# Moving the low weight parts and the rotation of a two-block transformer kernel to VectorE, and pairing the first two outputs of each residual projection

## The chip, the cores and the metric

The kernel runs on one core of a Trainium2 chip. The metric is the device time of one execution in microseconds (us): the median of three runs is 2573.86 us (2573.84 to 2576.16). A change of less than 0.2%, about 5 us, can hardly be told from none.

## The reference

Two blocks work on one sequence of 512 tokens with 1024 channels, all in float32. The first block mixes three branches (gated linear attention "GLA" with 4 heads, a short convolution, sliding-window attention), gates and merges them, and runs a feed-forward network. The second block has two layers, each with sparse attention (an indexer picks the top keys), a gated recurrence ("HGRN") with 4 heads, a merge of both, and a feed-forward network. Cut to what matters here:

```python
def first_block(x, ...):
    u = rmsnorm(h, g_mix); z = u @ w_in
    o = gla_chunked(q, k, v, log_a)          # q*exp(b-b_ref), k*exp(b_ref-b), chunks of 64
    merged = gate0 * (o @ w_gla_o) + gate1 * (conv @ w_conv_o) + gate2 * (swa @ w_swa_o)
    h = h + merged @ w_o
    h = h + (silu(hid[..., :D_FF]) * hid[..., D_FF:]) @ w_down
def second_block(x, ...):
    for l in range(2):
        proj = rmsnorm_2(x, norm_mix[l]) @ w_in[l]
        aq = apply_rope(rmsnorm_2(aq, q_norm), cos, sin)     # the same for ak; iq and ik without norm
        y_attn = dsa_attention(aq, ak, av, iq, ik, iw)       # top 128 keys of each query by an index score
        y_hgrn = hgrn2_chunked(q_h, k_in, v_h, log_f)
        x = x + (sig(ga) * (y_attn @ w_proj_attn) + sig(gb) * (y_hgrn @ w_proj_hgrn)) @ w_out
        x = x + (silu(g) * u) @ w_ffn_out

def apply_rope(x, cos, sin):
    x1, x2 = x[..., :half], x[..., half:]
    return concatenate([x1 * cos - x2 * sin, x2 * cos + x1 * sin])
```

## The kernel before

**Matmuls.** The kernel keeps float32 accuracy by splitting both operands in a high part (rounded to the fp32r type) and a low part (the rest). A product is then three matmuls: weight low by input high, weight high by input low, high by high. `project` does this for one output tile of 128 channels by 512 tokens, over 8 slices ("K tiles") of 128 input channels (22 for the down projections): 24 matmuls into one PSUM tile `mm`, of which there are four. `project_tokens` has the tokens on the partitions: it fills all four `mm` tiles at once, with 12 matmuls for each K tile.

**Weights.** `weights` loads a float32 tile `wraw` by a DMA on SyncE's queue, ScalarE copies it to fp32r (`whi`, line 149), and an engine subtracts that from the raw weights (`wlo`, line 152). Of each of the three tiles there are three buffers of 512 columns (`wraw`: 1024). One `whi`/`wlo` pair holds four K tiles of `project`, or one K tile of `project_tokens`. The engine for `wlo` comes from the list `self.lows`, in turn: `mixing()` sets GpSimd, GpSimd, VectorE; `feeding()` sets VectorE alone; while the index and `hv` projections are written, GpSimd and VectorE take turns; from the last gates of each final merge until the next `feeding()` GpSimd alone has it. In the profile GpSimd is POOL, VectorE DVE, ScalarE ACT, TensorE PE.

**Order.** Every engine executes its instructions in order. The order is made when the program is built: a scheduler walks through the instructions as written, with a priority, and places each where its model of the engines says that it can go; weight preparation and the reading of PSUM (`evict`) are written at high priority. The stages of the second block are written one after the other (`ORDER`: index and `hv` projections, index rotation, keys, key rotation, queries, values, query rotation, then selections and attention blocks, and HGRN behind them), but selection, attention and HGRN are interleaved on the engines.

**Rotation.** `rope` multiplies by a cosine table (GpSimd, line 799), takes two half-width products with a sine table (VectorE, lines 800 and 801) and adds (GpSimd, line 802). `rotate` does so for the four token tiles of keys (`akx`) or queries (`aqx`), while `rsqrt` (lines 229 to 233, ten small dependent operations on 128x32) makes the norm on VectorE, which then multiplies (line 825). The index rotation (line 802 into `idxr`, then the copy in line 858 on VectorE) has 320 columns in each token tile.

**GLA heads.** `gla_head` has three operations on GpSimd: lines 444, 447 (halves of `lvx`) and 454 (`rE`).

**HGRN heads.** `hgrn_head` goes back and forth between VectorE (lines 493, 497, 511) and GpSimd (lines 486, 494, 495) over seven levels.

**Residual.** `merge` makes eight tiles of merged channels and splits each in `mgh` (ScalarE, line 211) and `mgl` (VectorE, line 212). `residual` then calls `project` for each of eight output tiles; the K tiles of one output are these eight merged tiles, in order. Three residual projections have 8 K tiles (`w_o` and `w_out` in two layers), three have 22.

## Time and profile before

| | us |
|---|---|
| median of 3 runs | 2573.86 |
| the profiled execution, own time | 2573.17 |
| its span, first to last instruction | 2571.4 |
| PE busy | 2496.6 (97%) |
| DVE busy | 1366.3 (53%) |
| ACT busy | 1008.3 (39%) |
| POOL busy | 772.2 (30%) |

The profile shows one execution. "Busy" is the share of time in which an engine has at least one instruction under way; matmuls overlap, so a matmul's own duration (0.39 us) is longer than the distance from one to the next. The span falls into stages, of which these are spoken of below (in us from the start): GLA heads with sliding-window attention 100 to 250; the merge and the first residual projection around 450 to 500; layer 0 of the second block with the index stage near 900, the two rotations 941 to 1000, selection, attention and HGRN 1000 to 1200, and the merge after that; layer 1 with the same stages from 1740, 1784 to 1845 and 1850 to 2050. The rest is feed-forward, where PE is never idle.

### The profile page before, as it was taken

The page shows a single profiled execution, that of the slowest core. Times are in us where ns is not written, and L with a number is a line of the kernel's source. Part 1 is how long each engine was busy: PE and PEld are TensorE (multiplying, and loading weights), DVE is VectorE, ACT ScalarE, POOL GpSimd, SP SyncE. Part 2 cuts the span into 40 slices and gives each one's busy share as a digit, 9 for nine tenths or more (in the row PEclk, how much of TensorE's full clock was granted, in tenths as well). Part 3 has the DMA queues.
Part 4 walks back from the last instruction along what each step waited for, and adds up shares of the span by engine and source line. Part 5 has one row for each costly group of instructions (what it writes and reads, how often), then busy time and mean ns, then how long its engine had stood idle before and what let it go on. Part 6 is the DMA issues. An engine that isn't in the chain of part 4 may idle for free.

```text
span 2571.4 us, 31562 instructions
## 1 busy us (share of the span) xinstructions
PE 2496.6 (97%) x11742; PEld 2038.5 (79%) x11742; DVE 1366.3 (53%) x2572; ACT 1008.3 (39%) x1830; POOL 772.2 (30%) x672
## 2 busy tenths in 40 slices
PE   9999999999999998999999999999899999999999
PEld 7877888888888876777888888887677788888887
DVE  4675222477774547996244444333799724444432
ACT  5633333444443334443343333334454333433321
POOL 4234334511101254443351111015544435211100
PEclk9999999999999999999999999999999999999999
DMA  4112232322223222111222222322111032222232
GB/s 137 58 53 81 94 99 93 107 91 98 93 94 97 91 77 71 50 37 44 99 95 98 98 93 95 99 89 90 66 50 45 26 99 97 95 99 98 92 107 88
DMA packets 67434, 217.66 MB, mean 85 GB/s; under 512 B 7744, under 2 KB 8640, under 8 KB 67280
## 3 DMA queue, kind: packets, MB, share of 16 engines
q1 hardware_dynamic: 67280, 215.65, 25.3%
q8 instruction: 92, 1.51, 0.2%
q14 instruction: 62, 0.51, 0.1%
HBM read 213.52 MB, written 2.10 MB: 84 GB/s over the span
## 4 chain that ended last, share of the span: by engine, by line
PE 80%; DVE 12%; issue 3%; ACT 2%; POOL 2%; DMA 0%; SPq 0%; DVEq 0%; ACTq 0%; POOLq 0%
PE mm L194 23%; PE mm L195 23%; PE mm L193 23%; PE mm L168 2%; PE mm L169 2%; PE mm L170 2%; DVE wlo L152 1%; DVE score L885 1%; PE at L935 1%; PE at L923 1%; DVE m L884 1%; DVE rsq_w L232 1%; POOL hG L495 1%; PE at L239 1%; DVE rsq_w L231 1%
## 5 line engine op out<-in xcount | busy, mean ns | idle before, releaser
L149 ACT CAST whi<-wraw 128x512 fp32r<-128x512 f32 (+3 forms) x824 | 502.3, 610 | 1177.8 <-PE mm L195 949.9
L194 PE MATMUL mm<-xl,whi 128*128 128x512 f32 x1920 | 758.0, 395 | 0.0
L193 PE MATMUL mm<-xh,wlo 128*128 128x512 f32 x1920 | 757.3, 394 | 0.0
L195 PE MATMUL mm<-xh,whi 128*128 128x512 f32 x1920 | 755.8, 394 | 0.0
L152 DVE TENSOR_TENSOR wlo<-wraw,whi 128x512 fp32r<-128x512 f32 (+2 forms) x533 | 390.2, 732 | 508.3 <-ACT whi L149 505.6
L152 POOL TENSOR_TENSOR wlo<-wraw,whi 128x512 fp32r<-128x512 f32 (+2 forms) x291 | 377.4, 1297 | 747.7 <-ACT whi L149 705.6
L195 PEld LDWEIGHTS mm<-xh,whi 128*128 128x128 f32 x1920 | 361.2, 188 | 73.6 <-issue 1.7
L194 PEld LDWEIGHTS mm<-xl,whi 128*128 128x128 f32 x1920 | 361.1, 188 | 73.4 <-issue 1.7
L193 PEld LDWEIGHTS mm<-xh,wlo 128*128 128x128 f32 x1920 | 361.1, 188 | 72.3 <-issue 0.7
L193 PE MATMUL mm<-acth,wlo 128*128 128x512 f32 x528 | 205.4, 389 | 0.0
L194 PE MATMUL mm<-actl,whi 128*128 128x512 f32 x528 | 205.4, 389 | 0.0
L195 PE MATMUL mm<-acth,whi 128*128 128x512 f32 x528 | 205.4, 389 | 0.0
L733 POOL TENSOR_TENSOR fg<-fg,rstd 128x512 f32<-128x512 f32 x44 | 56.6, 1287 | 425.9 <-ACT fg L732 425.9
L168 PE MATMUL mm<-wlo,xh 128*128 128x512 f32 (+2 forms) x384 | 147.0, 383 | 34.6 <-DVE wlo L152 23.1
L170 PE MATMUL mm<-whi,xh 128*128 128x512 f32 (+2 forms) x384 | 144.8, 378 | 0.0
L169 PE MATMUL mm<-whi,xl 128*128 128x512 f32 (+2 forms) x384 | 144.4, 376 | 0.1
L202 DVE TENSOR_TENSOR gate<-mm,rstd 128x512 f32<-128x512 f32 x56 | 38.7, 691 | 151.2 <-PE mm L195 150.4
L277 POOL TENSOR_TENSOR acc<-acc,sq 128x512 f32<-128x512 f32 x39 | 58.8, 1508 | 199.3 <-ACT sq L274 198.3
L168 PEld LDWEIGHTS mm<-wlo,xh 128*128 128x128 f32 x384 | 73.6, 192 | 54.5 <-DVE wlo L152 26.4
L193 PEld LDWEIGHTS mm<-acth,wlo 128*128 128x128 f32 x528 | 99.1, 188 | 20.6
L194 PEld LDWEIGHTS mm<-actl,whi 128*128 128x128 f32 x528 | 99.1, 188 | 20.6
L195 PEld LDWEIGHTS mm<-acth,whi 128*128 128x128 f32 x528 | 99.1, 188 | 20.6
(356 smaller groups left out, 3336.4 us busy)
## 6 DMA issues: line engine op xcount, KB each, us to landing
wraw<-in_w_ffn_in SPq DMA_DIRECT2D x88, 512.0 KB, 3.2
wraw<-in_w_gate SPq DMA_DIRECT2D x56, 512.0 KB, 3.2
wraw<-in_w_in SPq DMA_DIRECT2D x52, 512.0 KB, 3.2
wraw<-in_w_up SPq DMA_DIRECT2D x44, 512.0 KB, 3.2
wraw<-in_w_tok SPq DMA_DIRECT2D x32, 512.0 KB, 3.2
wraw<-in_w_ffn_out SPq DMA_DIRECT2D x32, 512.0 KB, 3.5
wraw<-in_w_down SPq DMA_DIRECT2D x16, 512.0 KB, 3.5
wraw<-in_w_po SPq DMA_DIRECT2D x32, 256.0 KB, 2.6
```

The lines of the kernel that those rows point to most:

```text
L149: nc.scalar.copy(wh, raw[:, k:k + m, :])
L152: eng.tensor_tensor(wl, raw[:, k:k + m, :], wh.bitcast(F32), op=OP.subtract)
L168: nc.tensor.matmul(ps[t][:, 0:w], xh, wl, start=i == 0, stop=False)
L169: nc.tensor.matmul(ps[t][:, 0:w], xl, wh, start=False, stop=False)
L170: nc.tensor.matmul(ps[t][:, 0:w], xh, wh, start=False, stop=i == KD - 1)
L193: nc.tensor.matmul(ps, wl, xh, start=i == 0, stop=False)
L194: nc.tensor.matmul(ps, wh, xl, start=False, stop=False)
L195: nc.tensor.matmul(ps, wh, xh, start=False, stop=i == n - 1)
L202: self.nc.vector.tensor_tensor(out, ps, other, op=OP.mult)
L231: nc.vector.tensor_tensor(w, v, y, op=OP.mult)
L277: (nc.vector if d % 2 and len(acc) > 1 else nc.gpsimd).tensor_tensor(a, a, sq, op=OP.add)
L733: nc.gpsimd.tensor_tensor(g, g, self.rstd, op=OP.mult)
```

## The change

The change does four things. (1) `feeding()` is called before the GLA heads, and the calls of `mixing()` and the special list for the index and `hv` projections are gone, so that from the GLA heads on all `wlo` subtractions go to VectorE, but for the ends of the three final merges and the residual projections behind them, which stay on GpSimd. Of 291 such instructions on GpSimd 73 stay there (25 of them before the GLA heads), and 218 go to VectorE. (2) Both GpSimd operations of `rope` go to VectorE: 48 instructions. (3) The three GpSimd operations of `gla_head` go to VectorE: 12 instructions. (4) `residual`, where it has 8 K tiles, makes its first two outputs together in the new `project_pair`: K tiles 0 to 3 of the first output, 0 to 3 of the second, 4 to 6 of the first, 4 to 6 of the second, then K tile 7 of both. Their weights come in four DMAs of 256 KB where two of 512 KB stood.

```diff
+    def project_pair(self, srcs, X):
+        nc = self.nc
+        n = len(X)
+        pss = [self.mm() for _ in srcs]
+        ws = [[] for _ in srcs]
+
+        def products(j, ks):
+            for i in ks:
+                (wh, wl), (xh, xl) = ws[j][i], X[i]
+                nc.tensor.matmul(pss[j], wl, xh, start=i == 0, stop=False)
+                nc.tensor.matmul(pss[j], wh, xl, start=False, stop=False)
+                nc.tensor.matmul(pss[j], wh, xh, start=False, stop=i == n - 1)
+
+        for k in range(0, n, 4):
+            for j, src in enumerate(srcs):
+                ws[j] += self.weights(src[:, k:k + 4, :], 4)
+                products(j, range(k, min(k + 4, n - 1)))
+        for j in range(len(srcs)):
+            products(j, (n - 1,))
+        return pss
...
-        nc.gpsimd.tensor_tensor(Xc[:, :, 0:64], mid, Bc[:, :, 0:64], op=OP.subtract)
+        nc.vector.tensor_tensor(Xc[:, :, 0:64], mid, Bc[:, :, 0:64], op=OP.subtract)
...
-        nc.gpsimd.tensor_tensor(Xc[:, :, 0:64], Xc[:, :, 0:64], kc[:, :, 0:64], op=OP.mult)
+        nc.vector.tensor_tensor(Xc[:, :, 0:64], Xc[:, :, 0:64], kc[:, :, 0:64], op=OP.mult)
...
-        nc.gpsimd.tensor_tensor(E, E, q, op=OP.mult)
+        nc.vector.tensor_tensor(E, E, q, op=OP.mult)
...
         ygla = []
+        self.feeding()
         for hd in range(4):
...
     def residual(self, src, X, scale=1.0):
+        got = {}
+
         def update(d):
-            ps = self.project(src[d], X)
+            if len(X) == KD and d < 2:
+                if d == 0:
+                    got.update(enumerate(self.project_pair([src[0], src[1]], X)))
+                ps = got.pop(d)
+            else:
+                ps = self.project(src[d], X)
...
-        nc.gpsimd.tensor_tensor(o, xv, b(C, 64), op=OP.mult)
+        nc.vector.tensor_tensor(o, xv, b(C, 64), op=OP.mult)
...
-        nc.gpsimd.tensor_tensor(out, o, o2, op=OP.add)
+        nc.vector.tensor_tensor(out, o, o2, op=OP.add)
...
         for c in ORDER:
-            self.mixing()
-            if c in "xh":
-                self.lows = [nc.gpsimd, nc.vector]
...
         for l in range(2):
-            self.mixing()
             M = self.second_mix(l, X)
```

The order of the instructions moves with it. On DVE at the key rotation of layer 0 (`akss` is the sum of squares, `akx` a token tile of the keys, `tabC` and `tabS` the cosine and sine tables) there stood before:

```order
L813 TENSOR_REDUCE akss<-asq 128x8 x2
L800 TENSOR_TENSOR rope_7750<-akx,tabS 128x8x32
L813 TENSOR_REDUCE akss<-asq 128x8 x2
L801 TENSOR_TENSOR rope_7750<-akx,tabS 128x8x32
L820 TENSOR_SCALAR akss<-akss 128x32
L800 TENSOR_TENSOR rope_7757<-akx,tabS 128x8x32
L152 TENSOR_TENSOR wlo<-wraw,whi 128x512
L229 TENSOR_SCALAR rsq_y<-akss 128x32
L801 TENSOR_TENSOR rope_7757<-akx,tabS 128x8x32
```

and now (the shifted line numbers 842, 828, 829, 830, 831 are 813, 799, 800, 801, 802 of before):

```order
L842 TENSOR_REDUCE akss<-asq 128x8 x2
L152 TENSOR_TENSOR wlo<-wraw,whi 128x512
L842 TENSOR_REDUCE akss<-asq 128x8 x2
L828 TENSOR_TENSOR rope_7753<-akx,tabC 128x512
L849 TENSOR_SCALAR akss<-akss 128x32
L829 TENSOR_TENSOR rope_7754<-akx,tabS 128x8x32
L152 TENSOR_TENSOR wlo<-wraw,whi 128x512
L250 TENSOR_SCALAR rsq_y<-akss 128x32
L830 TENSOR_TENSOR rope_7754<-akx,tabS 128x8x32
L252 TENSOR_TENSOR rsq_w<-akss,rsq_y 128x32
L828 TENSOR_TENSOR rope_7760<-akx,tabC 128x512
L152 TENSOR_TENSOR wlo<-wraw,whi 128x512
```

The cosine products and sums have joined DVE's row, and a `wlo` stands in every third to ninth place, eight from the first sum of squares to the end of the rotation.

On PE at the first residual projection (`mgh_3900` is the last of the eight merged tiles) the first output ended, and the second began, like this before:

```order
L193 MATMUL mm_3905<-mgh_3875,wlo_3913 128x512
L194 MATMUL mm_3905<-mgl_3876,whi_3912 128x512
L195 MATMUL mm_3905<-mgh_3875,whi_3912 128x512
L193 MATMUL mm_3905<-mgh_3900,wlo_3913 128x512
L194 MATMUL mm_3905<-mgl_3901,whi_3912 128x512
L195 MATMUL mm_3905<-mgh_3900,whi_3912 128x512
L193 MATMUL mm_3946<-mgh_3611,wlo_3950 128x512
```

and now the last tile is taken by both, one behind the other:

```order
L207 MATMUL mm_3906<-mgh_3875,wlo_3961 128x512
L208 MATMUL mm_3906<-mgl_3876,whi_3960 128x512
L209 MATMUL mm_3906<-mgh_3875,whi_3960 128x512
L207 MATMUL mm_3905<-mgh_3900,wlo_3946 128x512
L208 MATMUL mm_3905<-mgl_3901,whi_3945 128x512
L209 MATMUL mm_3905<-mgh_3900,whi_3945 128x512
L207 MATMUL mm_3906<-mgh_3900,wlo_3961 128x512
```

So 42 matmuls stand ahead of the first that reads the last merged tile, where 21 stood.

On PE at the start of layer 0's first merge (`yhh` and `yhl` are the HGRN heads' outputs, `aL`, `aPT` and `av` belong to an attention block, `rS` and `AT` to a HGRN head) the merge began behind all attention work before:

```order
L407 MATMUL at<-rS,hf 128x128
L405 MATMUL at<-hv,AT 128x128
L407 MATMUL at<-rS,hf 128x128
L193 MATMUL mm<-xh,wlo 128x512
L194 MATMUL mm<-xl,whi 128x512
L195 MATMUL mm<-xh,whi 128x512
```

and now attention and a HGRN head still run among the merge's first products (line 960 is 931 of before, 964 is 935, 426 is 405, 428 is 407):

```order
L193 MATMUL mm<-yhh,wlo 128x512
L428 MATMUL at<-rS,hf 128x128
L426 MATMUL at<-hv,AT 128x128
L960 MATMUL at<-csts,aL 128x128 x4
L428 MATMUL at<-rS,hf 128x128
L426 MATMUL at<-hv,AT 128x128
L428 MATMUL at<-rS,hf 128x128
L194 MATMUL mm<-yhl,whi 128x512
```

In both layers the end of selection, attention and HGRN (a whole HGRN head in layer 0, two in layer 1) has moved in among the products of the first merge.

## Rows read from the trace of the kernel before

**Rows 1.** The page's part 1: busy us (share of the span) xinstructions
```profile
PE 2496.6 (97%) x11742; PEld 2038.5 (79%) x11742; DVE 1366.3 (53%) x2572; ACT 1008.3 (39%) x1830; POOL 772.2 (30%) x672
```

**Rows 2.** Waits of PE, whole span: us in total, times, longest
```profile
PE mm L168 <- DVE wlo L152: 23.1, 7, 7.7
PE mm L168 <- POOL wlo L152: 7.3, 4, 2.7
PE at L464 <- POOL lvx L447: 3.5, 4, 1.1
PE at L437 <- DVE gD L434: 3.3, 3, 1.1
```

**Rows 3.** Windows: length, PE, PEld, DVE, ACT, POOL busy (instructions), PEclk, DMA, GB/s
```profile
941.00:1000.00 59.00, 46.73 (x194) 36.09 (x193) 45.00 (x59) 21.33 (x47) 37.65 (x26) 0.91 0.18 63
1000.00:1200.00 200.00, 190.69 (x1088) 148.74 (x1087) 172.05 (x437) 97.63 (x207) 87.17 (x98) 1.00 0.13 44
1200.00:1310.00 110.00, 110.00 (x488) 90.58 (x487) 35.02 (x63) 36.61 (x60) 39.51 (x31) 1.00 0.30 96
1784.00:1845.00 61.00, 47.31 (x202) 36.95 (x201) 44.92 (x59) 21.51 (x48) 38.17 (x27) 0.94 0.20 69
1850.00:2050.00 200.00, 190.31 (x1075) 147.60 (x1075) 176.86 (x454) 100.31 (x208) 89.57 (x97) 0.99 0.12 41
100.00:250.00 150.00, 140.96 (x761) 116.45 (x760) 94.73 (x225) 60.80 (x131) 52.59 (x44) 1.00 0.18 61
```

**Rows 4.** Timeline of DVE in the key rotation: start, us, engine, line, operation
```profile
958.10 1.28 DVE L231 TENSOR_TENSOR rsq_w<-akss,rsq_y 128x32 f32<-128x32 f32 x1
959.30 0.41 DVE L801 TENSOR_TENSOR rope<-akx,tabS 128x256 f32<-128x256 f32 x1
959.64 0.18 DVE L232 SCALAR_TENSOR_TENSOR rsq_w<-rsq_w,rsq_y 128x32 f32<-128x32 f32 x1
...
961.26 1.20 DVE L232 SCALAR_TENSOR_TENSOR rsq_w<-rsq_w,rsq_y 128x32 f32<-128x32 f32 x1
```

**Rows 5.** Timeline of POOL in the same microseconds
```profile
957.76 1.57 POOL L802 TENSOR_TENSOR akx<-rope,rope 128x512 f32<-128x512 f32 x1
...
961.14 1.27 POOL L152 TENSOR_TENSOR wlo<-wraw,whi 128x512 fp32r<-128x512 f32 x1
```

**Rows 6.** Timeline of PE behind the query rotation; in brackets idle time and releaser
```profile
993.49 0.79 PE L168 MATMUL mm<-wlo,xh 128*128 128x512 f32 x1 [7.69 <-DVE wlo L152]
994.09 0.63 PE L169 MATMUL mm<-whi,xl 128*128 128x512 f32 x1
...
996.64 0.41 PE L169 MATMUL mm<-whi,xl 128*128 128x512 f32 x1
```

**Rows 7.** Timeline of DVE in the index stage of layer 0
```profile
904.57 0.83 DVE L858 COPY idxr<-idxr 128x64 f32<-128x64 f32 x1 [0.75 <-POOL idxr L802]
905.32 0.68 DVE L152 TENSOR_TENSOR wlo<-wraw,whi 128x512 fp32r<-128x512 f32 x1
```

**Rows 8.** Timeline of PE behind that subtraction
```profile
906.06 0.50 PE L168 MATMUL mm<-wlo,xh 128*128 128x512 f32 x1 [2.95 <-DVE wlo L152]
```

**Rows 9.** Timeline of PE at the first residual projection's last K tile
```profile
473.52 0.50 PE L193 MATMUL mm<-mgh,wlo 128*128 128x512 f32 x1 [0.93 <-ACT mgh L211]
474.25 0.50 PE L194 MATMUL mm<-mgl,whi 128*128 128x512 f32 x1 [0.22 <-DVE mgl L212]
```

**Rows 10.** Timeline of DVE in a GLA head
```profile
154.16 1.71 DVE L434 TENSOR_TENSOR gD<-gD,gk 128x512 f32<-128x512 f32 x1
```

**Rows 11.** Line 152 from 1000 to 1200 us: count, ns min/median/max
```profile
L152 POOL TENSOR_TENSOR wlo<-wraw,whi x22: 1259/1287/1457, 1001.5 to 1187.7; 128x512 fp32r<-128x512 f32 x22
...
L152 DVE TENSOR_TENSOR wlo<-wraw,whi x10: 674/682/1221, 1007.4 to 1169.1; 128x512 fp32r<-128x512 f32 x10
```

**Rows 12.** Waits of DVE and of POOL, 1000 to 1200 us
```profile
DVE wlo L152 <- ACT whi L149: 8.1, 1, 8.1
...
POOL wlo L152 <- ACT whi L149: 81.7, 17, 13.6
```

## The prediction

> **What bounds the kernel now.** I read the page's first part first: PE is busy in 2496.6 of 2571.4 us [rows 1]. So everything that the change can win lies in the 74.8 us in which PE is idle, and in stretches in which PE runs at a lower clock; everything it can lose is new idle time of PE. The list of what PE waits for says whose fault the idle time is [rows 2]: 30.4 us are waits of the first matmul of a token projection (line 168) for low weight parts, 23.1 of them for VectorE's; 3.5 and 3.3 us are GLA heads waiting for `lvx` and `gD`. The busy times by stretch say where [rows 3]: the two rotation stretches lose 59.00 - 46.73 = 12.3 and 61.00 - 47.31 = 13.7 us; selection, attention and HGRN ("the dense stretches") lose 9.3 and 9.7 us; the GLA stretch 9.0; the first merge of layer 0 (1200 to 1310) nothing.
>
> Why VectorE is late in the rotations is seen in single instructions. The same small operation on 128x32 takes 0.18 us at one time and 1.20 us at another [rows 4], and at the slow times GpSimd has a two-input operation under way (1.57 us from 957.76, 1.27 us from 961.14 [rows 5]): VectorE's operation ends when GpSimd's does. So the ten small steps of the norm, which are alone worth some 2 us, are stretched behind one GpSimd operation after another, and the `wlo` that PE wants stands behind them in VectorE's row. PE then waits 7.69 us in one piece [rows 6]. And it pays once more: the matmuls behind that gap start 0.425 us apart (994.09 to 996.64, six steps) where a dense stretch has 110.00 us / 488 = 0.225 us [rows 3, 6]; that is the lower clock level of the two, 1.2 instead of 2.4 GHz, after idle time. The stretches' mean granted clock is 0.91 and 0.94 [rows 3].
>
> The Trainium skill has a rule for what rows 4 and 5 show ("SBUF — State Buffer", "Who interferes with whom"): a VectorE instruction with two SBUF inputs contends with a GpSimd instruction that reads SBUF, and the later one is blocked entirely, not slowed. The trace agrees: 1.20 us beside GpSimd against 0.18 us without.
>
> **The change, part by part.** Forecasts are made against the profiled execution, 2573.2 us (span 2571.4 and 1.8 around it); it lies 0.7 us under the median of the runs, which I neglect.
>
> (a) The rotations of keys and queries. GpSimd loses the cosine products, the sums and the `wlo`, so that only zero fills are left on it here. What VectorE now has in one rotation: 24 wide operations (4 sums of squares, 4 cosine products, 4 sums, 4 norm products, 8 `wlo`), 8 half-width ones and 11 small ones. A wide one takes 0.68 us [rows 11]; successive ones overlap by about 0.07 us (the half-width one of 0.41 us at 959.30 is followed at 959.64 [rows 4]), so 0.61. The sum: 24 x 0.61 + 8 x 0.34 + 11 x 0.20 = 14.6 + 2.7 + 2.2 = 19.5 us. PE has meanwhile one token projection to do: 8 K tiles of 12 matmuls, 96 x 0.225 = 21.6 us. So VectorE keeps up, by 2 us only, provided that the `wlo` come in time. The new order puts a `wlo` in every third to ninth place; the longest piece between two (two wide, two half-width and four small operations, and the `wlo` itself) is about 3.3 us, against 2.7 us in which PE uses up one K tile, and three buffers let VectorE run ahead. So I take nearly all of the 26.0 us of idle time, and the lower clock behind it: six steps x 0.2 us = 1.2 us, at three places in the trace (959, 994 and 1836 us; one stands in the rows), 3.6. Of these 29.6 us I leave 1.6 for the evacuation of the four PSUM tiles. **Gain 28 us**; bounds 14 (every second gap stays) and 29.6.
>
> (b) The index rotation and the index and `hv` weights. At 905.32 a `wlo` stands behind a copy that waited 0.75 us for GpSimd's sum [rows 7], the last of several such exchanges, and PE waits 2.95 us for it [rows 8]. On one engine the exchange is gone. Line 168's waits of 30.4 us [rows 2] are 26.0 in the rotations, so at most 4.4 us are left for these stages. **Gain 3.5 us**; bounds 0 and 4.4. The low parts of the index weights now stand among the norm's small steps at each layer's start; there they replace GpSimd operations that block VectorE, so I set nothing for them.
>
> (c) The GLA heads. `gD` takes 1.71 us [rows 10] where an undisturbed wide operation takes 0.68 [rows 11], and PE waits 3.3 us for it in three heads and 3.5 us for `lvx` from GpSimd in four [rows 2]. Now `lvx` has two more operations of 0.34 us on VectorE and `rE` one of 0.61, but the order puts `gD` ahead of `dec`, `rD` and the scan. VectorE's load there is 94.7 of 150 us [rows 3], so the moved `wlo` have room. **Gain 4 us** of the 6.8; bounds -2 (VectorE's row has a `wlo` ahead of `gD`) and 7.
>
> (d) The pair of residual outputs. PE waits 0.93 and 0.22 us for the last merged tile [rows 9]; with 21 matmuls more in between (21 x 0.225 = 4.7 us) it is there. The same gap stands at three residual projections, one in the rows: 3 x 1.15. The four `mm` tiles suffice (two are held), the DMA bytes are the same. **Gain 3 us**; bounds 0 and 3.5.
>
> (e) The dense stretches. Here the change costs. 22 `wlo` per stretch go from GpSimd to VectorE [rows 11] (I take the same number in layer 1): 22 x 0.61 = 13.4 us on top of 172.05 and 176.86 us of 200 [rows 3], so 185.5 and 190.3. PE's own busy time there is 190.7 and 190.3 us [rows 3]: VectorE becomes as long as PE. Two things relieve it: the new order pushes the last HGRN heads and attention blocks in among the first merge's products, where VectorE has 35.0 of 110 us [rows 3], and GpSimd's 22 operations of 1.29 us no longer block VectorE or stand in front of GpSimd's own HGRN steps. Bounds: a gain of half of the idle 19.0 us, 9.5; a loss of all of the moved work, 2 x 13.4 = 27 us. I take a small **loss of 4 us**, 2 per layer: the load is equal to PE's and not above it, and the row of PE is filled with merge products.
>
> (f) Merges and feed-forward. In the merge stretch PE has no idle time, VectorE 35.0 of 110 us [rows 3]; more `wlo` there cost nothing. The feed-forward already has all `wlo` on VectorE.
>
> Sum: 28 + 3.5 + 4 + 3 - 4 = 34.5; 2573.2 - 34.5 = 2538.7, say **2539 us**, 1.4% faster.
>
> **The rivals.**
>
> A. VectorE becomes the bound in the dense stretches. Priced by the upper bound of (e): 27 us lost instead of 4, 2562 us. For it: 96% of PE's time before any wait inside a row that alternates with GpSimd and PE. Against it: the spill into the merge.
>
> The Trainium skill speaks for A ("Perfetto Trace Analysis", "Optimizing Scalar/DVE Operations"): where VectorE is saturated, offloading work, even to GpSimd, may make sense, though the shared read port may take the gain away. By its first half the `wlo` of these stretches belong on GpSimd, which is rival A's time; the trace bears out the second half, in rows 4 and 5.
>
> B. Slower than before: VectorE's row is held up by the `wlo` themselves. An engine executes in order, and a `wlo` waits for ScalarE's `whi`, which waits for PE to free a buffer. On GpSimd these waits are 81.7 us in the first dense stretch, 17 of 22 instructions [rows 11, 12]; there they hurt little, on VectorE they would hold the selection and HGRN behind them. If half of 81.7 us came onto PE's path in each of two layers, 82 us would be lost: 2539 + 82 - 4 = 2617. It ends slower than before from 47% of that, 38 us for both layers together. Against it: VectorE already has 10 `wlo` in that stretch, and waited for `whi` once, 8.1 us [rows 12], at the stretch's start.
>
> C. The rotation doesn't do what it should: VectorE's row stays the wall. If a whole rotation without `wlo` (19.5 - 8 x 0.61 = 14.6 us) ran ahead of the next `wlo`, three buffers would cover 3 x 2.7 = 8.1 us, and PE would wait 6.5 us in each of four rotations: 26 us, so that (a) gives 3.6 instead of 28: 2563 us. Against it stands the order, which interleaves.
>
> **How the numbers follow.** My forecast has 0.72, A 0.13, C 0.07, B 0.05; 0.03 is for causes that I don't see. The range reaches down to 2525 (half of the dense idle time gone: 2539 - 4 - 9.5) and up to 2559 (most of A, or half of (a) with (c) and (b) near zero). A run can tell about 0.2%, 5 us, from no change: faster than 2569 holds my forecast, A and C, 0.91; the same 0.04; slower 0.05.
>
> **What would show it.** In the profile after, the PE gaps of 7.69 us and the half-clock matmuls behind the rotations are gone, the 128x32 steps all take about 0.2 us, and line 168's waits for `wlo` fall from 30 us to under 5. The gap ahead of the last merged tile is gone at all three places. POOL's busy time falls by about 218 x 1.29 + 48 rotation operations, some 340 us, with PE's unchanged within 10. VectorE is over 90% busy in the dense stretches. I am wrong if PE's idle time in the dense stretches doubles (A), if VectorE waits there for `whi` in many pieces (B), or if line 168 still waits for `wlo` behind rotation work (C).

## The result, and the profile after

The changed kernel takes 2531.8 us (median; 2530.59 to 2532.61) beside 2574.39 for the kernel before (now four runs): a ratio of 0.9834, 95% interval 0.9818 to 0.9849, so 1.7% faster. The forecast was 2539 with a range of 2525 to 2559. The profiled execution has a span of 2530.5 us, 40.9 less than the 2571.4 of the kernel before.

The page's part 1 of the kernel after answers [rows 1] (busy us, share of the span, instructions):

```profile
PE 2493.2 (99%) x11742; PEld 2041.8 (81%) x11742; DVE 1454.1 (57%) x2850; ACT 1003.2 (40%) x1826; POOL 424.3 (17%) x394
```

POOL's busy time has fallen by 347.9 us (some 340 were expected), PE's has changed by 3.4. PE's idle time has halved, from 74.8 to 37.3 us (span less busy time). What PE still waits for, in the view of its waits over the whole span (us in total, times, longest), answers [rows 2]:

```profile
PE at L530 <- DVE lvx L514: 6.6, 16, 1.2
PE at L260 <- DVE ron L436: 6.1, 4, 2.8
PE mm L193 <- DVE wlo L152: 3.4, 3, 1.5
PE mm L193 <- ACT yhh L232: 3.0, 2, 1.5
...
PE mm L168 <- DVE wlo L152: 0.9, 1, 0.9
```

The 30.4 us for which line 168 waited are 0.9, and these stand at the kernel's start, as they did before. The waits for `gD` and for GpSimd's `lvx` of the GLA heads are gone. At the top stand waits of the HGRN heads (`lvx`, the normalised output `ron`, and its high part `yhh`) and of the products around them (`wlo` at line 193).

The rotation of the keys in the timeline of DVE (start, us, engine, line, operation) answers [rows 4]. Every 128x32 step takes 0.18 us now, between wide operations of 0.68 us and a `wlo` every few places:

```profile
933.84 0.18 DVE L252 TENSOR_TENSOR rsq_w<-akss,rsq_y 128x32 f32<-128x32 f32 x1
933.94 0.69 DVE L828 TENSOR_TENSOR rope<-akx,tabC 128x512 f32<-128x512 f32 x1
934.54 0.68 DVE L152 TENSOR_TENSOR wlo<-wraw,whi 128x512 fp32r<-128x512 f32 x1
935.15 0.18 DVE L253 SCALAR_TENSOR_TENSOR rsq_w<-rsq_w,rsq_y 128x32 f32<-128x32 f32 x1
935.25 0.68 DVE L831 TENSOR_TENSOR akx<-rope,rope 128x512 f32<-128x512 f32 x1
```

Where the 40.9 us come from is read by stages. A stage runs from its first matmul to the next stage's, and its length comes from windows laid on these points. "Token" is index, `hv`, keys, queries and values with their rotations; "dense" is selection, attention, HGRN and the first merge, up to the second merge's first product on the attention's output. Here are the windows of the kernel after, token and dense stage of layer 0, then of layer 1 (length; PE, PEld, DVE, ACT and POOL busy; granted clock; the DMA columns behind it are not used):

```profile
863.20:973.80 110.60, 109.49 (x529) 91.30 (x528) 71.09 (x180) 48.45 (x100) 2.03 (x4) 1.00 0.29 94
973.80:1252.80 279.00, 266.34 (x1401) 209.51 (x1400) 214.79 (x520) 120.19 (x243) 56.52 (x71) 0.98 0.17 56
...
1696.40:1804.90 108.50, 107.81 (x519) 90.09 (x518) 62.89 (x152) 47.12 (x98) 1.05 (x2) 1.00 0.29 96
1804.90:2083.00 278.10, 266.01 (x1401) 210.54 (x1400) 214.73 (x520) 119.69 (x243) 62.10 (x76) 0.98 0.17 55
```

The same four stages of the kernel before:

```profile
874.50:1006.00 131.50, 114.45 (x529) 92.66 (x529) 74.60 (x131) 48.49 (x100) 66.94 (x58) 0.96 0.23 79
1006.00:1277.00 271.00, 261.69 (x1401) 207.05 (x1400) 196.17 (x482) 119.09 (x243) 107.42 (x114) 1.00 0.17 58
1722.00:1848.70 126.70, 111.25 (x519) 90.62 (x518) 64.05 (x103) 47.14 (x98) 65.64 (x58) 0.97 0.24 82
1848.70:2122.50 273.80, 264.11 (x1401) 208.26 (x1400) 196.73 (x482) 124.73 (x247) 113.98 (x118) 0.99 0.17 56
```

So the token stages win 20.8 and 18.2 us by the first matmuls' own times (39.0 together), and the dense stages lose 8.0 and 4.3. The first stage, up to the first residual, wins 10.0; the three residual stages 1.4, 1.3 and 1.4. Feed-forward and second merges stay within 0.1 us.

The dense stages' loss is seen at the end of the last HGRN head. The timeline of PE of the kernel after, layer 0 (idle time and releaser in brackets):

```profile
1182.85 0.40 PE L195 MATMUL mm<-yhh,whi 128*128 128x512 f32 x1
1186.07 0.66 PE L260 MATMUL at<-csts,ron 128*128 128x128 f32 x4 [2.82 <-DVE ron L436]
1188.22 1.65 PE L193 MATMUL mm<-yhh,wlo 128*128 128x512 f32 x3 [1.49 <-ACT yhh L232]
1189.66 0.63 PE L194 MATMUL mm<-yhl,whi 128*128 128x512 f32 x1
1190.09 0.63 PE L195 MATMUL mm<-yhh,whi 128*128 128x512 f32 x1
...
1193.81 0.80 PE L193 MATMUL mm<-xh,wlo 128*128 128x512 f32 x1 [1.38 <-DVE wlo L152]
```

PE has run out of other products, waits 2.82 us for `ron` and 1.49 for its high part, and the matmuls behind that start 0.43 us apart instead of 0.23: half clock. In the window from 1187 to 1199 us the granted clock (behind POOL's busy time) is 0.57:

```profile
1187.00:1199.00 12.00, 9.40 (x24) 6.97 (x25) 5.07 (x8) 2.87 (x5) 0.00 (x0) 0.57 0.18 66
```

### The profile page after: what moved, and what is told of

Same layout as the page of the kernel before. It is cut to its first block, busy times and chain, and to the rows that moved or that the text cites. A ratio compares the mean times of both kernels' runs of the same rounds, so it can differ in the third digit from the quotient of the medians.

```text
span 2530.5 us, 31512 instructions
## 1 busy us (share of the span) xinstructions
PE 2493.2 (99%) x11742; PEld 2041.8 (81%) x11742; DVE 1454.1 (57%) x2850; ACT 1003.2 (40%) x1826; POOL 424.3 (17%) x394
## 4 chain that ended last, share of the span: by engine, by line
PE 91%; DVE 4%; ACT 2%; issue 1%; POOL 1%; DMA 0%; SPq 0%; DVEq 0%; POOLq 0%; ACTq 0%
PE mm L193 25%; PE mm L194 25%; PE mm L195 25%; PE mm L168 3%; PE mm L169 3%; PE mm L170 3%; PE at L964 1%; PE at L952 1%; PE at L260 1%; PE at L960 1%; PE at L530 1%; DVE hf L518 1%; DVE wlo L152 1%; PE at L580 0%; PE at L609 0%
## 5 line engine op out<-in xcount | busy, mean ns | idle before, releaser
L152 DVE TENSOR_TENSOR wlo<-wraw,whi 128x512 fp32r<-128x512 f32 (+2 forms) x751 | 537.4, 716 | 551.0 <-ACT whi L149 547.3
L152 POOL TENSOR_TENSOR wlo<-wraw,whi 128x512 fp32r<-128x512 f32 (+1 forms) x73 | 95.8, 1315 | 91.7 <-ACT whi L149 73.8
L714 POOL TENSOR_TENSOR acc<-acc,gate 128x512 f32<-128x512 f32 x20 | 33.7, 1687 | 342.3 <-DVE gate L709 342.3
```

The costliest lines, as they stand in the source:

```text
L152: eng.tensor_tensor(wl, raw[:, k:k + m, :], wh.bitcast(F32), op=OP.subtract)
L714: eng.tensor_tensor(acc[m], acc[m], g, op=OP.add)
```

## The experiments

The theories after the result were two. First, in the token stages GpSimd's two-input operations and VectorE's shut each other out, and the low parts behind them come late; the rivals are the order and the exchange of results inside the rotation. Second, the dense stages pay for VectorE's load; the rivals are the low parts' own waits, and the last head's place. Here are the stage lengths (us) of all kernels; "first" ends at the first residual.

```
                       first  token 0  dense 0  token 1  dense 1   median
before                 467.7    131.5    271.0    126.8    273.8   2574.4
after                  457.7    110.7    279.0    108.5    278.1   2531.8
rotation alone         468.0    111.8    271.1    109.4    273.8   2536.6
low parts alone        467.3    119.2    279.1    113.2    278.7   2556.7
GLA and pair alone     464.0    133.5    270.9    127.8    274.7   2567.6
after + 8 reads        459.0    125.1    279.5    121.7    277.3   2560.9
after + fills          458.8    110.6    277.0    108.6    280.0   2533.1
after, merges swapped  458.4    110.6    277.6    108.5    279.6   2531.6
after, HGRN lows back  457.8    110.7    269.3    108.6    268.9   2513.9
  and load elsewhere   458.2    110.7    269.3    108.4    269.4   2517.4
  and load in place    458.6    110.6    277.2    108.5    274.1   2526.7
  heads 1, 2 only      458.0    110.6    271.9    108.5    272.7   2521.6
  heads 3, 4 only      458.4    110.7    269.3    108.5    270.4   2515.8
  all on GpSimd        458.8    110.7    269.0    108.5    270.1   2514.9
```

Each row is one profiled execution. Kernels whose dense stages have the same work as the kernel after (low parts alone, 8 reads, fills) lie between 277.0 and 279.5 us in layer 0 and between 277.3 and 280.0 in layer 1, so there a difference of under 3 us says little. The token stages with both parts of the change and no added reads agree within 0.2 us; those of the kernel before and of "GLA and pair alone", which have the same work, differ by 2.0 and 1.0.

**The parts alone.** The rotation's two operations on VectorE, in the kernel before:

```diff
-        nc.gpsimd.tensor_tensor(o, xv, b(C, 64), op=OP.mult)
+        nc.vector.tensor_tensor(o, xv, b(C, 64), op=OP.mult)
...
-        nc.gpsimd.tensor_tensor(out, o, o2, op=OP.add)
+        nc.vector.tensor_tensor(out, o, o2, op=OP.add)
```

> The kernel before with one part of the change alone: the rotation's cosine product and its sum (lines 799 and 802) on VectorE; the low weight parts stay where they were, two of three on GpSimd. Theory (two-input GpSimd operations block VectorE, and the exchange between the two engines inside a rotation makes the low parts late): the 39.0 us that the change takes from the two token-projection stages need both parts, since each remaining low part on GpSimd (1.29 us) still blocks VectorE; some 15 to 25 us of the 39.0 come, so 2548 to 2559 us, and PE's idle time in the two stages falls from 32.5 to 12 to 20 us. Rival (the exchange of the rotation alone is the cause): nearly all of the 39.0 comes, 2535 to 2540 us, idle under 5 us. Rival (the low parts alone are the cause): under 5 us come, 2569 us or more. In all three the GLA stage (15.4 us idle), the residuals (45.1 us each) and the dense stretches (9.3 and 9.7 us idle) stay as before.

Measured: 2536.56 us, ratio 0.9852 (0.9838 to 0.9867). The token stages win 37.1 of the 39.0 us, so the first rival was right and my sum of two halves wrong. The low parts that stay on GpSimd cost 1.9 us in both layers together. It is not that they don't collide: VectorE's 128x32 steps still take up to 1.3 us here. The timeline of POOL in this kernel shows a `wlo` that is held up for 4.53 us:

```profile
976.14 4.53 POOL L152 TENSOR_TENSOR wlo<-wraw,whi 128x512 fp32r<-128x512 f32 x1 [1.23 <-ACT whi L149]
```

The timeline of DVE in the same kernel and the same microseconds shows operation upon operation, the next one started before the last has ended, up to 979.5 us. The one behind that takes 1.67 us instead of 0.68, while GpSimd's `wlo` ends (976.14 + 4.53 = 980.67):

```profile
976.37 1.28 DVE L825 TENSOR_TENSOR aqx<-aqx,rsq_y 128x512 f32<-128x512 f32 x2
977.57 0.68 DVE L802 TENSOR_TENSOR aqx<-rope,rope 128x512 f32<-128x512 f32 x1
978.17 0.41 DVE L800 TENSOR_TENSOR rope<-aqx,tabS 128x256 f32<-128x256 f32 x1
978.51 0.68 DVE L825 TENSOR_TENSOR aqx<-aqx,rsq_y 128x512 f32<-128x512 f32 x1
979.11 0.41 DVE L801 TENSOR_TENSOR rope<-aqx,tabS 128x256 f32<-128x256 f32 x1
979.55 1.67 DVE L802 TENSOR_TENSOR aqx<-rope,rope 128x512 f32<-128x512 f32 x1
```

So here it is GpSimd that is kept out first, and PE had enough other `wlo` meanwhile: its wait at line 168 for `wlo` is 0.9 us, as in the kernel after.

The low parts alone, in the kernel before (the first line stands ahead of the GLA heads):

```diff
+        self.feeding()
...
         for c in ORDER:
-            self.mixing()
-            if c in "xh":
-                self.lows = [nc.gpsimd, nc.vector]
...
         for l in range(2):
-            self.mixing()
```

> The kernel before with the other part alone: every low weight part on VectorE wherever the change puts it there; rotation, GLA operations and residuals as before. Theory: GpSimd has only the rotation's two operations per head group left, but VectorE's low parts stand behind them in its row; in the token stages 10 to 20 of the 39.0 us come. The dense stretches lose what the change loses there, 12.2 us in the sum of both layers, since the same low parts move. The GLA stage gains some 3 of its 9.7 us. In all 2565 to 2575 us: the same as before. Rival (the low parts alone are the cause): token stages gain 30 us or more and the whole 2545 to 2552. Rival (VectorE's row is now held up by GpSimd's sums, and no GpSimd low part can be served meanwhile): token stages lose, and the whole is over 2580 us.

Measured: 2556.71 us, ratio 0.9932 (0.9917 to 0.9946), under the 2565 of the theory. The token stages win 25.9 us, more than the 10 to 20 of the theory and less than the rival's 30. With 37.1 for the rotation alone the two sum to 63 where both together give 39.0: either one takes away most of the loss. What the theory said is seen, though smaller: low parts stand behind stretched steps. PE's waits at line 168 in this kernel are 9.5 us:

```profile
PE mm L168 <- DVE wlo L152: 9.5, 7, 2.4
...
PE at L464 <- POOL lvx L447: 6.7, 3, 2.3
```

and 128x32 steps take up to 1.33 us, as GpSimd's sums run beside them. In the dense stages this kernel loses 8.1 and 4.9 us: the whole change's loss there (8.0 and 4.3) is the low parts'.

The GLA operations and the pair of outputs, in the kernel before (lines 444, 447 and 454 on VectorE, and `project_pair`):

> The kernel before with the two parts that lie in separate stages: the three operations of a GLA head on VectorE (seen in the first stage, up to the first residual), and the pair of residual outputs (seen in the three residual stages). Theory for the first stage: its 9.7 us of gain come from the waits for gD and lvx, so from these three operations; 5 to 9 us here. Rival: they come from the low parts of that stage, which stay on GpSimd here; then under 3 us. The residuals: 1.3 us each, 3.9 in all, as with the whole change. Everything else as before. In all 2561 to 2566 us by the theory, 2567 to 2571 by the rival.

Measured: 2567.64 us, ratio 0.9974 (0.9964 to 0.9983). The residual stages are 43.9 us each, as in the kernel after: the pair is worth 1.4 us a time. The first stage wins 3.7 us, between theory and rival; the low parts alone win 0.4 there, both together 10.0. Each takes away one of the two waits of [rows 2] and leaves or lengthens the other. Of the GLA operations alone the view of PE's waits shows

```profile
PE at L458 <- DVE gD L455: 3.7, 3, 1.3
```

(3.3 us before), and with the low parts alone the wait for `lvx` is 6.7 us, as shown above (3.5 before). Most of the gain comes only when both are gone. Why `gD` is late with VectorE's three operations alone was not followed further.

**The shared reads.** Useless work on the changed kernel, once in each key and query projection, on a scratch tile that has been read:

```diff
             nc.vector.reduce_sum(ss[:, t * 8:(t + 1) * 8], sq, axis=AX.X)
+            if t == NT - 1:
+                c = self.cos2[:, 0, None, :].to_broadcast([P, 8, 64])
+                nc.gpsimd.tensor_tensor(sq, sq, c, op=OP.mult)
+                for _ in range(7):
+                    nc.gpsimd.tensor_tensor(sq, sq, c, op=OP.mult)
```

> The changed kernel with useless work added: after the last sum of squares of each key and query projection, GpSimd multiplies a scratch tile by a cosine table eight times in place (two-input operations on 128x512 which read SBUF; some 1.3 to 1.7 us each, 10 to 14 us a rotation), while VectorE does the rotation. Nobody waits for the result. In the kernel before, the rotation's own eight GpSimd operations took 11 to 13 us there. Theory (GpSimd's reads of SBUF block VectorE, and this alone makes the low parts late): VectorE's 19.5 us a rotation and these 12 make 31 where PE has 21.6; the token stages, 110.7 and 108.5 us, grow by 10 to 20 us in the sum of both, and the whole is 2542 to 2552. Rival (it is the exchange inside the rotation, VectorE waiting for GpSimd's sum and GpSimd for VectorE's products, and not the port): VectorE stretches, but PE waits under 2 us, and the whole is 2531 to 2535.

In the control the last line is `nc.gpsimd.memset(sq, 0.0)`, seventeen times.

> The control for the run with eight useless GpSimd multiplications: at the same place one such multiplication and seventeen zero fills of the same tile, which write SBUF and read nothing (0.52 us each for 128x512 in the kernel before, 9 us in all), useless as well. Theory (what blocks VectorE is a GpSimd operation that reads two inputs): no loss, 2530 to 2534 us, and VectorE's 128x32 steps stay at 0.2 us. Rival (any GpSimd work beside VectorE slows it): a loss near that of the eight multiplications, 10 us or more.

Measured: 2560.92 us, ratio 0.995 (0.9935 to 0.9965), with the eight multiplications (some 1.5 us each, 12.4 a rotation); 2533.06 us, 0.9839 (0.9824 to 0.9853), with one multiplication and the fills (10.6 us a rotation). The multiplications cost 14.4 and 13.2 us in the token stages, in sum more than the theory's 10 to 20, the fills nothing. The instructions of `rsq_w`, the norm's steps on 128x4 and 128x32, in the kernel with the multiplications (ns min/median/max):

```profile
L253 DVE SCALAR_TENSOR_TENSOR rsq_w<-rsq_w,rsq_y x54: 144/163/1289, 136.0 to 2045.3; 128x4 f32<-128x4 f32 x42, 128x32 f32<-128x32 f32 x12
```

and in the kernel with the fills:

```profile
L253 DVE SCALAR_TENSOR_TENSOR rsq_w<-rsq_w,rsq_y x54: 143/161/181, 135.8 to 2016.0; 128x4 f32<-128x4 f32 x42, 128x32 f32<-128x32 f32 x12
```

A step of 0.18 us becomes 1.29 beside GpSimd operations that read, though they exchange nothing with VectorE. PE's wait at line 168 for `wlo` is 0.9 us with the fills; with the multiplications it is

```profile
PE mm L168 <- DVE wlo L152: 19.2, 7, 4.7
```

That reads alone can make the low parts late is thereby shown; the exchange isn't needed. How much of the 39.0 us the exchange had in the kernel before is not shown, since there it and the reads come from the same operations.

**The dense stages.** The changed kernel with the HGRN projections' low parts back on GpSimd, two of three:

```diff
         hv = self.hv
+        self.mixing()
         yh = []
...
+        self.feeding()
         acc = self.merge(A["w_gate2"][l, 1], X, A["w_po"][l, 1], yh, None, 2, False, self.i)
```

> The changed kernel with the low parts of the dense stretches' HGRN projections back as they were, two of three on GpSimd, and the rest on VectorE. The changed kernel's dense stretches with the first merge take 278.7 and 277.8 us, 7.9 and 4.3 more than before. Theory (VectorE's load of 22 low parts more per stretch is the cost): both stretches come back to 271 to 274 us, the whole is 2520 to 2525. Rival (the cost is the last HGRN head, whose serial steps now end behind the merge products and leave PE idle and at half clock at the merge): VectorE's load decides less, the stretches stay at 276 us or more, and the whole is 2527 to 2533. Rival (GpSimd's low parts block VectorE there as they do in the rotations): the stretches grow by some 5 us each, and the whole is over 2538.

Measured: 2513.92 us (2513.1 to 2514.39), ratio 0.9765 (0.975 to 0.9779): 17.9 us faster than the changed kernel; none here is faster. It is the smaller part of what the change had moved: of 38 low parts that run in each dense stage 14 are back, and those of the first merge stay on VectorE. The stages are 9.7 and 9.2 us shorter than after, and shorter than before too. Its dense stages in the windows:

```profile
973.90:1243.20 269.30, 261.90 (x1401) 206.87 (x1400) 207.94 (x506) 119.47 (x243) 76.01 (x90) 1.00 0.18 58
1795.30:2064.30 269.00, 261.72 (x1402) 206.69 (x1401) 209.82 (x506) 124.68 (x247) 82.60 (x94) 1.00 0.18 57
```

VectorE is 6.9 and 4.9 us less busy, PE loses no clock. Where the 9.7 us of layer 0 lie is seen when the stage is split 195 us behind its start. The kernel after:

```profile
973.80:1168.80 195.00, 190.46 (x1063) 148.26 (x1061) 174.42 (x448) 97.79 (x207) 50.66 (x65) 1.00 0.14 46
1168.80:1203.80 35.00, 26.88 (x125) 20.67 (x125) 20.52 (x44) 7.39 (x12) 5.86 (x6) 0.85 0.14 47
```

and this one:

```profile
973.90:1168.90 195.00, 188.82 (x1079) 147.23 (x1078) 173.84 (x447) 95.96 (x205) 76.01 (x90) 1.00 0.13 43
1168.90:1203.90 35.00, 33.78 (x152) 27.09 (x151) 18.89 (x37) 11.63 (x19) 0.00 (x0) 1.00 0.27 83
```

In the first 195 us PE is even busier in the kernel after. In the 35 us behind them PE is idle for 8.1 us instead of 1.2 and at a granted clock of 0.85 instead of 1.00; so the loss is made at the end of the last head (in layer 1 the same: 27.60 us busy at 0.86, against 34.74 at 1.00). Is it the load, or the low parts' own waits? One useless VectorE operation beside each of the low parts that are back, which sums a constant:

> The changed kernel with the dense stretches' low parts back on GpSimd (2513.9 us; stretches 269.3 and 268.9 us), and beside each of these 15 low parts per layer one useless VectorE operation of the same length (a sum over 128x512, 0.68 us), which waits for nothing and for which nobody waits. It puts back the load, 15 x 0.68 = 10.2 us of VectorE per layer, without the low parts' own waits. Theory (the loss there is VectorE's load): the stretches grow back to 276 to 279 us each, the whole is 2527 to 2534. Rival (the loss is that a low part in VectorE's row waits for ScalarE's high part and holds up the row, or that PE waits for it behind the row's other work): the stretches stay at 268 to 271 us, the whole is 2512 to 2517.

Measured: 2517.42 us, but the operations ran at 526.7 to 572.2 us, in the feed-forward, and the run says nothing of the question. Tied to the raw weights they stay in place:

```diff
                 eng.tensor_tensor(wl, raw[:, k:k + m, :], wh.bitcast(F32), op=OP.subtract)
+                if eng is nc.gpsimd and getattr(self, "dense", False):
+                    nc.vector.reduce_sum(self.junk[:, 0:m], raw[:, k:k + m, :], axis=AX.X)
```

> The useless VectorE operations of the run before stood at 527 to 572 us, in the feed-forward, and so put no load on the dense stretches (269.3 and 269.4 us). Here each is tied to its place: it sums the raw weights from which GpSimd makes the low part beside it (128x512, about 0.68 us, 16 per layer, 10.9 us), needs only the landed transfer, and nobody waits for it. Everything else as in the kernel with the dense low parts back on GpSimd (2513.9 us, stretches 269.3 and 268.9 us, VectorE busy 207.9 and 209.8 us there). Theory (the loss of 9.7 and 9.2 us against that kernel is VectorE's load): the stretches grow to 276 to 280 us, the last HGRN head's first transpose, 191 us behind the stretch's start, comes at 200 us or later, the whole is 2527 to 2534 us. Rival (it is the low part's own wait for ScalarE's high part in VectorE's row): the stretches stay at 268 to 272 us, the whole is 2512 to 2519 us.

Measured: 2526.67 us, ratio 0.9817 (0.9802 to 0.9832). The stages grow by 7.9 and 5.2 us, so the load without the low parts' own waits brings back 81% and 57% of the difference (of the 16 sums a layer 12 and 14 run inside the stage, and they wait 2.3 us in all for their transfers); the last head's first transpose comes 201.8 and 200.7 us behind the stage's start. The tail is there again, in the timeline of PE of this kernel:

```profile
1184.35 0.50 PE L195 MATMUL mm<-yhh,wlo 128*128 128x512 f32 x1 [1.51 <-DVE wlo L152]
1187.13 0.66 PE L262 MATMUL at<-csts,ron 128*128 128x128 f32 x4 [0.44 <-DVE ron L438]
1189.28 1.65 PE L195 MATMUL mm<-yhh,wlo 128*128 128x512 f32 x3 [1.50 <-ACT yhh L234]
```

What the remaining 1.8 and 4.0 us are (the first is within the scatter; the waits for `whi`, or another order of PE's work, which each of these kernels has), the run doesn't tell.

Then which low parts? `self.mixing()` for the first two heads and `self.feeding()` for the others, and the other way round:

> The changed kernel with two of three low parts of the first two HGRN heads of each layer back on GpSimd (8 per layer); those of the last two heads stay on VectorE. In the changed kernel the second head's first transpose comes 115 us behind the stretch's start, where the kernel with all of them back has 101 us, so 13 of the 12 to 14 us by which the last head is late arise between the first and the second head, where VectorE is busy 47.8 and 45.8 of 50 us. Theory (VectorE is the bound there): these 8 give back nearly all, the stretches come to 269 to 272 us, the whole to 2513 to 2519. Rival (each low part costs the same wherever it stands): half comes back, 274 us each, 2521 to 2524.

> The other half: two of three low parts of the last two HGRN heads of each layer back on GpSimd, those of the first two on VectorE. Theory (VectorE is the bound between the first and the second head): under 3 us per layer come back, the stretches stay at 275 to 279 us, the whole at 2525 to 2531. Rival (each low part costs the same wherever it stands): half comes back, 274 us each, 2521 to 2524. Rival (what counts is VectorE's row at the end, ahead of the last head's serial steps): nearly all comes back, 2513 to 2519.

Measured: 2521.64 us (ratio 0.9797, 0.9782 to 0.9812) and 2515.77 (0.9771, 0.9757 to 0.9786). The first two heads' 8 low parts give back 7.1 and 5.4 us, the last two heads' 9.7 and 7.7, of 9.7 and 9.2. My theory that the time is lost between the first and second head fell. The sum of the two exceeds the whole, so it is no price per instruction; the last rival (what counts is VectorE's row ahead of the last head's end) was nearest. But for the kernel before, the kernels order, within the scatter, by when the last `ron` is transposed, behind the stage's start:

```
                       last ron (us)     stage (us)
all on GpSimd          197.7  199.2     269.0  270.1
two of three back      201.4  200.5     269.3  268.9
heads 3, 4 only        201.9  204.7     269.3  270.4
heads 1, 2 only        208.7  209.6     271.9  272.7
load in place          212.8  211.1     277.2  274.1
after                  212.6  213.8     279.0  278.1
before                 199.3  202.0     271.0  273.8
```

Up to some 202 us the head's end is covered; seven us later the stage is some 3 us longer, eleven us later 5 to 10. That is a comparison of kernels, each with its own order, and no test of that one time. The kernel before stands apart, 2 and 5 us above the kernel with two of three back at about the same end; its further low parts on GpSimd and other waits were not taken apart.

> The changed kernel with every low part of the HGRN projections on GpSimd (24 per layer, where the kernel at 2513.9 us has two of three). It asks how far the relief goes. Theory (VectorE is the bound in the first 100 us of a dense stretch and GpSimd has room, 29 of 76 us busy at the start): VectorE loses another 8 x 0.68 = 5.4 us, PE's idle time in the stretches, 7.4 and 7.3 us, falls by 1 to 4 us each, the whole is 2506 to 2512. Rival (a GpSimd low part of 1.3 to 1.7 us keeps VectorE from the port about as long as it spares it): no change, 2512 to 2517; or PE waits for GpSimd's low parts, 2518 or more.

Measured: 2514.88 us, ratio 0.9769 (0.9753 to 0.9785): no change against two of three, the rival's case. That fits an end that is covered: it gains nothing by coming earlier.

Last, the two merges swapped in the changed kernel:

```diff
-        acc = self.merge(A["w_gate2"][l, 1], X, A["w_po"][l, 1], yh, None, 2, False, self.i)
-        return self.merge(A["w_gate2"][l, 0], X, A["w_po"][l, 0], yattn, acc, 4, True)
+        acc = self.merge(A["w_gate2"][l, 0], X, A["w_po"][l, 0], yattn, None, 2, False, self.i)
+        return self.merge(A["w_gate2"][l, 1], X, A["w_po"][l, 1], yh, acc, 4, True)
```

> The changed kernel with the two merges of the second block swapped: the first merge is on the attention's outputs, the last on HGRN's. In the changed kernel the last HGRN head ends late, its serial steps leave PE gaps of up to 2.8 us at the start of the merge on its output, and matmuls at half clock behind them (10 us in layer 0, 10 in layer 1). Theory (the dense stretches' 12.2 us are the tail of that last head, put there by VectorE's longer row): with the merge on attention first, the tail is covered by it, and 6 to 12 us come back: 2520 to 2526. Rival (VectorE's load as such, spread over the stretch): under 3 us, 2529 to 2533; or the attention's last block is now the tail, and it is slower, 2535 or more.

Measured: 2531.57 us, ratio 0.983 (0.9815 to 0.9845), no gain in the median, with runs from 2526.0 to 2533.7: the theory of the swap fell. In the profiled one, in layer 0, the gaps only move to the end of the attention's last block, in the timeline of PE of this kernel:

```profile
1150.65 0.85 PE L960 MATMUL at<-csts,aL 128*128 128x128 f32 x4 [1.70 <-ACT aL L956]
1152.23 1.97 PE L964 MATMUL at<-av,aPT 128*128 128x64 f32 x8 [0.73 <-ACT aPT L962]
```

and the granted clock is 0.57 over 1150 to 1162 us. That either end is late because both stand in one row on VectorE is my reading, not shown by this run.

## Why the prediction was right, and where its terms were off

The forecast was 34.5 us of gain; the profiled spans differ by 40.9. The sign held, and so did the mechanism of the rotations. But four terms were mis-sized, three too small by 14.6 us together and one by 8.3 the other way; that the sum came so near is in part luck.

(a) and (b), the rotations and the index stage: 31.5 us forecast, 39.0 measured in the two token stages. The idle time was judged well: 30.7 us of it went (17.05 to 1.11 and 15.45 to 0.69), and I had some 28. What was too small is the price of a wait beyond its idle time: PE's busy time fell by 8.4 us, and I had 3.6 from "six steps" at three places. The rows to read were the windows around these places in the kernel before (busy times, then granted clock):

```profile
959.10:962.50 3.40, 3.25 (x9) 2.03 (x7) 3.26 (x7) 0.10 (x1) 2.78 (x3) 0.50 0.00 0
985.80:993.49 7.69, 0.01 (x1) 0.00 (x0) 7.59 (x10) 0.62 (x1) 6.56 (x5) 0.76 0.00 0
993.49:996.70 3.21, 3.21 (x8) 2.53 (x9) 1.75 (x3) 0.00 (x0) 0.00 (x0) 0.50 0.47 163
1835.90:1839.80 3.90, 3.85 (x9) 3.09 (x10) 1.80 (x3) 0.00 (x0) 0.00 (x0) 0.50 0.41 139
```

At half clock PE worked for 3.25 + 3.21 + 3.85 = 10.3 us (9, 8 and 9 matmuls in the rows, where I had six steps each), of which half, 5.2 us, is lost. The clock is low already in a part of the 7.69 us of waiting (0.76 on the mean), but there PE has no work that it could lengthen. The other 3.2 us were not taken apart; a first matmul behind a wait takes 0.50 to 0.80 us instead of 0.39. The mechanism that I read from [rows 4, 5] was confirmed by the run with useless reads and its control. But I charged rotation and low parts alike, and the rotation alone gives 37.1 us. My reading is that a late GpSimd low part has others behind which PE can run, while a late rotation holds the `wlo` in its own row. No run separates this from the spacing: alone on GpSimd the low parts mostly start 3 to 7 us apart, while in the key rotation of the kernel before GpSimd pauses for only 0.5 us in the 15.3 us from 947.1 on. Rival C (the rotation stays the wall) fell: 0.9 us of waits at line 168, none of it in the rotations. One reading was loose: the 26.0 us are all of PE's idle time in the two windows. Line 168's waits for `wlo` are 25.2 of it, and 0.9 of the 30.4 stand at the kernel's start, so 4.3 were left for (b), not 4.4.

The Trainium skill ("SBUF — State Buffer", "Who interferes with whom") has for GpSimd that only an operation which reads SBUF contends with VectorE's two-input ones; the trace agrees, 1.29 us beside reads and 0.18 beside fills.

(c) the GLA heads: 4 us forecast, 10.0 measured, above my upper bound of 7. I counted two waits, 6.8 us, and left 2.8 of them for operations newly on VectorE. Both went entirely. I didn't count the waits for `AT` (1.0 us to none) and `ron` (1.3 to 0.4) and 0.9 us of PE's busy time. A start of the kernel that was 0.8 us shorter (3.5 to 2.7 us for `lbe`, between 2.6 and 3.7 in these runs) is scatter and not the change.

(d) the pair: 3 us forecast, 1.4 + 1.3 + 1.4 = 4.1 measured, above my bound of 3.5; the waits themselves were 3.5 (2.8 for `mgh` and 0.7 for `mgl`).

(e) the dense stages: a loss of 4 us forecast, 12.3 measured, within the bounds of -9.5 and 27. The step that failed is the relief: "the new order pushes the last HGRN heads ... in among the first merge's products". It does, but those products are then used up. In the kernel after the first product of `yhh` comes 170.2 and 153.7 us behind the stage's start, before 194.1 and 192.5; and the last head's first transpose comes at 202.4 and 203.0 us, before at 188.4 and 191.5. When the head's serial steps end, nothing is left to cover them. I weighed loads over a stage, where one end decided. The load was mis-sized too: I moved 22 low parts a layer, counted in 200 us, where 38 move in the whole stage, and VectorE's busy time in it grew by 18.6 and 18.0 us instead of 13.4. Rival A's mechanism, VectorE as the bound, was thus at work, at less than half of its price of 27 us. PE's idle time in the two stages grew from 9.3 and 9.7 us to 12.7 and 12.1, so it didn't double; the rest of the loss, 4.6 and 1.9 us, is longer busy time, with a granted clock of 0.98 over either stage where the kernel before has 1.00 and 0.99. My sign that VectorE is over 90% busy came out in part only: in the first 195 us of layer 0's stage it is busy 174.4 us, 89%. In the windows of the kernel after it is busy 47.78 us of the 50 from 1000 on, and 35.58 of the last 50, where PE is idle:

```profile
1000.00:1050.00 50.00, 49.24 (x277) 39.27 (x276) 47.78 (x132) 27.83 (x59) 14.88 (x19) 1.00 0.13 45
...
1150.00:1200.00 50.00, 41.27 (x214) 32.30 (x214) 35.58 (x76) 12.53 (x24) 12.05 (x14) 0.90 0.13 46
```

The Trainium skill ("Perfetto Trace Analysis", "Optimizing Scalar/DVE Operations") says that work of a saturated VectorE may go even to GpSimd, but that it might not help, as the two share a read port. By the runs it does help here: 16 low parts a layer back on GpSimd are worth 17.9 us in both layers together.

Rival B (VectorE's row held up by `wlo` that wait for `whi`) fell: in the first 200 us of layer 0's dense stage these waits are 4.4 us in 5 pieces, where [rows 12] have 8.1 in one, and in layer 1 7.5 us in 9 pieces, before 9.9 in 2: more pieces, less time, and far from the 41 us a layer of its price.

(f) Merges and feed-forward: nothing forecast, within 0.1 us per stage measured.

## What to carry to other kernels

Put an operation on GpSimd by what stands behind it: a low part with spares behind it can wait, a step of a chain whose engine also feeds PE can't. Where two engines exclude each other, test with useless work that nobody waits for, and with a control that only writes; and price half-clock stretches from windows by PE's busy time in them times the missing share of the clock, since a low clock costs nothing while PE waits. Where a stage ends in a serial tail, ask what product is left to cover it, not how busy its engines are on average.

## What was not expected

VectorE keeps GpSimd out as well: a `wlo`, elsewhere 1.29 us, took 4.53 on GpSimd while VectorE ran two-input operations nose to tail. Two causes that each look like half of a loss gave 37.1 and 25.9 of 39.0 us alone. And VectorE operations with no input from their own stage were placed a whole feed-forward ahead of where they were written (526.7 to 572.2 us instead of behind 974), which is how the first load test missed its place.
